# RoPE on half of each head: one row of the last tile split over GpSimd's DMA queue

## The chip, the cores and the metric

The kernel runs on one core of a Trainium2 chip. The metric is the device time of one execution in microseconds (us); the kernel before took 161.63 us, the median of three runs (161.6 to 161.7).

## What is computed

The input x is float32 of shape 16 x 512 x 16 x 64 (batch, position, head, dimension), and cos and sin are 512 x 32. Of the 64 values of a head, the first 32 (x1) are rotated and the last 32 (x2) are handed on untouched:

```python
rotated_first  = x1[..., :16] * cos[..., :16] - x1[..., 16:] * sin[..., :16]
rotated_second = x1[..., :16] * sin[..., :16] + x1[..., 16:] * cos[..., :16]
out = concatenate([rotated_first, rotated_second, x2], axis=-1)
```

Only the first 16 columns of cos and sin are used, and they depend on the position alone. x and the output have 33.55 MB each.

## The kernel before

The 8192 rows (batch times position) of 4 KB (16 heads of 64 floats) are cut into four tiles (`T`). A tile has 128 partitions, and each partition holds 16 consecutive rows (`K`), 64 KB that are contiguous in DRAM. The tiles live in `ring`, which has three slots (`NS`); tile 3 takes the slot of tile 0.

GpSimd's DMA queue first loads the two tables, 32 runs of 2 KB each (L63, L64). SyncE's queue loads tile 0, tile 1 and the first half (8 rows, `KC`) of tile 2 (L55). VectorE spreads the tables over the partitions (L73 to L83) and then rotates in place. `rotate` takes some of the 16 rows of a tile: two products (L96 into PSUM, L97 in place), a difference (L98) and a sum (L101) over the first 32 values of each head. The other 32 values ride along in the same slot, from the load to the store.

The order on the queues is the order of the program, with waits where data or a slot is needed. On SyncE: store of tile 0 (after its rotation), second half of tile 2, load of tile 3 (which waits until the store of tile 0 has landed), store of tile 1, store of tile 3. The store of tile 1 is held back by a dependency written by hand until 13 of 16 rows (`KM`) of tile 2 are rotated. On GpSimd: the two tables and the store of tile 2. Tiles 0, 1 and 3 are rotated in two halves of 8 rows, tile 2 in 8, 5 and 3 rows. The kernel ends when the store of tile 3 and the store of tile 2 have landed.

Of the kernel before, what the change touches and what calls it, by code (L numbers as in the profile page):

```python
# [1 line left out]

# [4 lines left out]


@with_exitstack
def kernel(  # L10
    ctx: ExitStack,
    tc: tile.TileContext,
    x: bass.AP,
    cos: bass.AP,
    sin: bass.AP,
    out: bass.AP,
):
    nc = tc.nc
    fp32 = mybir.dt.float32
    P = 128  # L20
    B, S, H, D = x.shape
    Q = D // 4
    HF = D // 2

    K = 16
    T = B * S // (P * K)
    PB = S // K
    REP = P // PB  # L30
    R = H * D
    NS = 3
    KC = K // 2
    KM = 13

    xf = x.rearrange("b s h d -> (b s h d)").rearrange("(t p f) -> t p f", t=T, p=P)
    of = out.rearrange("b s h d -> (b s h d)").rearrange("(t p f) -> t p f", t=T, p=P)
    cosf = cos.rearrange("(p k) j -> p (k j)", k=K)
    sinf = sin.rearrange("(p k) j -> p (k j)", k=K)

    const_pool = ctx.enter_context(tc.tile_pool(name="const", bufs=1))
    b_pool = ctx.enter_context(tc.tile_pool(name="bp", bufs=1, space=bass.MemoryType.PSUM))


    ring = const_pool.tile([P, NS, K, H, D], fp32)
    stage = const_pool.tile([P, 2, K, HF], fp32)
    spun = const_pool.tile([P, 2 * K, Q], fp32)
    packed = const_pool.tile([PB, 2 * K, Q], fp32)
    table = const_pool.tile([P, 2, K, 2, Q], fp32)

    def rows(t, lo, hi):
        return ring[:, t % NS, lo:hi].rearrange("p k h d -> p (k h d)")

    def load(t, lo=0, hi=K):
        return nc.sync.dma_start(out=rows(t, lo, hi), in_=xf[t, :, lo * R : hi * R])  # L55

    def store(t, lo=0, hi=K, queue=nc.sync):
        return queue.dma_start(out=of[t, :, lo * R : hi * R], in_=rows(t, lo, hi))  # L58


    nc.vector.memset(stage[:, :, :, 0:Q], 0.0)  # L61
    spread = stage.rearrange("(j b) t k i -> j b t (k i)", b=REP)
    nc.gpsimd.dma_start(out=spread[:, 0, 0], in_=cosf)  # L63
    nc.gpsimd.dma_start(out=spread[:, 0, 1], in_=sinf)  # L64
    load(0)
    load(1)
    load(2, 0, KC)

    PQ = PB // REP
    nc.vector.stream_shuffle(  # L73
        out=spun[:],
        in_=stage.rearrange("p t k j -> p (t k) j")[:, :, 0:Q],
        mask=[j % PQ * REP for j in range(PB)],
    )
    for q in reversed(range(REP)):
        n = PQ * (q + 1)
        nc.vector.tensor_copy(out=packed[0:n], in_=spun[q * PB : q * PB + n])  # L80

    for r in range(REP):
        nc.vector.tensor_copy(  # L83
            out=table[r * PB : (r + 1) * PB].rearrange("p t k c j -> p (t k) c j"),
            in_=packed.unsqueeze(2).to_broadcast((PB, 2 * K, 2, Q)),
        )
    C = table[:, 0].rearrange("p k c j -> p k (c j)")
    Sn = table[:, 1].rearrange("p k c j -> p k (c j)")

    def rotate(t, lo, hi):  # L90
        x1 = ring[:, t % NS, lo:hi, :, 0:HF]
        c = C[:, lo:hi].unsqueeze(2).to_broadcast((P, hi - lo, H, HF))
        s = Sn[:, lo:hi].unsqueeze(2).to_broadcast((P, hi - lo, H, HF))
        b_full = b_pool.tile([P, KC, H, HF], fp32, name="b_t")
        b_t = b_full[:, 0 : hi - lo]
        nc.vector.tensor_mul(out=b_t, in0=x1, in1=s)  # L96
        nc.vector.tensor_mul(out=x1, in0=x1, in1=c)  # L97
        nc.vector.tensor_sub(  # L98
            out=x1[:, :, :, 0:Q], in0=x1[:, :, :, 0:Q], in1=b_t[:, :, :, Q:HF]
        )  # L100
        return nc.vector.tensor_add(  # L101
            out=x1[:, :, :, Q:HF], in0=x1[:, :, :, Q:HF], in1=b_t[:, :, :, 0:Q]
        )

    rotate(0, 0, KC)
    rotate(0, KC, K)
    store(0)
    load(2, KC, K)
    load(3)
    rotate(1, 0, KC)  # L110
    rotate(1, KC, K)
    behind_loads = store(1)
    rotate(2, 0, KC)
    near = rotate(2, KC, KM)
    rotate(2, KM, K)
    store(2, queue=nc.gpsimd)

    tc.add_manual_dep(
        behind_loads.ins,
        near.ins.name,  # L120
        mybir.DependencyInfo(mybir.DependencyClass.Sync, mybir.DependencyReason.DATA),
        reason="the store follows the loads at the DMA engines",
    )
    rotate(3, 0, KC)
    rotate(3, KC, K)
    store(3)


# [1 line left out]
_INS = ['x', 'cos', 'sin']  # L130
_OUTS = [((16, 512, 16, 64), 'float32')]


# [23 lines left out]
```

## Time and profile before

| What | Value |
|---|---|
| Median of three runs | 161.63 us |
| Span of the profiled execution (first to last instruction) | 159.5 us; of this execution no time but the span is recorded |
| VectorE (DVE) busy | 112.9 us |
| GpSimd (POOL) busy | 1.9 us |
| Bytes moved by DMA | 67.24 MB, mean 422 GB/s |
| Transfers on SyncE's queue (q1) | 5 loads, 3 stores |
| Transfers on GpSimd's queue (q0) | 2 tables, 1 store |
| Store of tile 3 issued | 131.2 us, landing 27.4 us later |

The profile counts a DMA engine's work in packets. A packet is the piece of a transfer that one DMA engine carries out before it turns to another queue; its recorded time is given as a share of the time of all 16 engines in the stretch looked at. A packet is counted where it ends, so that a short stretch can show over 100%. "Landing" is the time from an issue until the transfer's completion has been counted on all its engines. A transfer's issue by an instruction and its movement by the DMA engines are thus two things: the first is shown on the issuing engine, the second in the queues.

### The profile page before, as it was taken

To read this page: it belongs to the slowest core of one execution; us is meant where nothing else is said; L and a number is where in the kernel's file an instruction comes from. 1 tells how busy PE (TensorE), PEld (TensorE's weight loads), DVE (VectorE), ACT (ScalarE), POOL (GpSimd) and SP (SyncE) were. 2 spreads that over 40 slices of the span, in tenths; PEclk is the share of its full clock that TensorE was granted. 3 is DMA by queue.
4 is the path that set the end of the run, shared out by engine and by line. 5 is a ranking of instruction groups with operands and counts; after the bars stand their busy time and mean duration, and the time that the engine had idled before them with its cause. 6 is when DMAs were issued, how large, how long until landed. Compare 5 with 4: busy or idle time off the path is not lost.

```text
span 159.5 us, 115 instructions
## 1 busy us (share of the span) xinstructions
DVE 112.9 (71%) x47; POOL 1.9 (1%) x7
## 2 busy tenths in 40 slices
DVE  1000959999999999999999999999999990000000
POOL 3000000000000000000000000010000000000000
DMA  7969979899699699699996996996996996998966
GB/s 263 542 263 542 444 345 526 362 427 526 271 493 551 263 526 526 263 395 427 493 526 263 526 526 263 526 526 263 526 526 263 526 510 279 526 427 362 526 263 263
DMA packets 1360, 67.24 MB, mean 422 GB/s; under 512 B 176, under 2 KB 176, under 8 KB 208
## 3 DMA queue, kind: packets, MB, share of 16 engines
q1 hardware_dynamic: 1152, 58.72, 85.7%
q0 software_dynamic: 208, 8.52, 12.4%
HBM read 33.69 MB, written 33.55 MB: 422 GB/s over the span
## 4 chain that ended last, share of the span: by engine, by line
DVE 61%; DMA 14%; issue 5%; DVEq 1%
DVE b_t L96 22%; DVE ring L97 22%; DMA ring<-in_x_dram 14%; DVE ring L101 10%; DVE ring L98 7%; DVEq L152 1%; DVEq L96 0%
## 5 line engine op out<-in xcount | busy, mean ns | idle before, releaser
L96 DVE TENSOR_TENSOR b_t<-ring,table 128x4096 f32<-128x4096 f32 (+2 forms) x9 | 35.6, 3959 | 2.1 <-DMA ring<-in_x_dram 1.9
L97 DVE TENSOR_TENSOR ring<-ring,table 128x4096 f32<-128x4096 f32 (+2 forms) x9 | 35.6, 3950 | 0.3
L98 DVE TENSOR_TENSOR ring<-ring,b_t 128x2048 f32<-128x2048 f32 (+2 forms) x9 | 18.4, 2050 | 0.3
L101 DVE TENSOR_TENSOR ring<-ring,b_t 128x2048 f32<-128x2048 f32 (+2 forms) x9 | 18.4, 2043 | 0.0
L73 DVE LOAD_MASK_SELECT spun<-stage x1 | 0.0, 14 | 14.4 <-DMA stage<-in_sin_dram 14.4
L83 DVE COPY table<-packed 32x1024 f32<-32x1024 f32 x4 | 2.7, 684 | 0.1
L58 POOL DMA_DIRECT2D out_dram<-ring x1 | 0.6, 559 | 101.7 <-DVE ring L101 101.7
L80 DVE COPY packed<-spun 32x512 f32<-32x512 f32 (+3 forms) x4 | 1.7, 416 | 0.1
L61 DVE MEMSET stage<- 128x512 f32 x1 | 0.5, 485 | 0.9 <-PEq L141 0.9
L73 DVE STREAM_SHUFFLE spun<-stage 128x512 f32<-128x512 f32 x1 | 0.7, 722 | 0.0
L63 POOL DMA_DIRECT2D stage<-in_cos_dram x1 | 0.6, 642 | 1.3 <-DVE stage L61 1.3
L64 POOL DMA_DIRECT2D stage<-in_sin_dram x1 | 0.5, 532 | 0.0
L141 POOL MEMSET const-bfloat16-1.0<- 128x1 bf16 x1 | 0.1, 101 | 0.0
L141 POOL MEMSET const-float32-0.0<- 128x1 f32 x1 | 0.1, 98 | 0.2 <-issue 0.2
L141 POOL MEMSET const-float32-1.0<- 128x1 f32 x1 | 0.1, 98 | 0.0
L141 POOL MEMSET const-uint8-127<- 128x1 uint8 x1 | 0.1, 98 | 0.0
## 6 DMA issues: line engine op xcount, KB each, us to landing
ring<-in_x_dram SPq DMA_DIRECT2D x2, 4096.0 KB, 40.7
stage<-in_cos_dram POOLq DMA_DIRECT2D x1, 64.0 KB, 8.9
stage<-in_sin_dram POOLq DMA_DIRECT2D x1, 64.0 KB, 13.3
ring<-in_x_dram SPq DMA_DIRECT2D x3, 28.9
out_dram<-ring SPq DMA_DIRECT2D x3, 27.4
out_dram<-ring POOLq DMA_DIRECT2D x1, 39.5
```

The lines of the kernel that those rows point to most:

```text
L58: return queue.dma_start(out=of[t, :, lo * R : hi * R], in_=rows(t, lo, hi))
L61: nc.vector.memset(stage[:, :, :, 0:Q], 0.0)
L63: nc.gpsimd.dma_start(out=spread[:, 0, 0], in_=cosf)
L64: nc.gpsimd.dma_start(out=spread[:, 0, 1], in_=sinf)
L73: nc.vector.stream_shuffle(out=spun[:], in_=stage.rearrange("p t k j -> p (t k) j")[:, :, 0:Q], mask=[j % PQ * REP for j in range(PB)],)
L80: nc.vector.tensor_copy(out=packed[0:n], in_=spun[q * PB : q * PB + n])
L83: nc.vector.tensor_copy(out=table[r * PB : (r + 1) * PB].rearrange("p t k c j -> p (t k) c j"), in_=packed.unsqueeze(2).to_broadcast((PB, ...
L96: nc.vector.tensor_mul(out=b_t, in0=x1, in1=s)
L97: nc.vector.tensor_mul(out=x1, in0=x1, in1=c)
L98: nc.vector.tensor_sub(out=x1[:, :, :, 0:Q], in0=x1[:, :, :, 0:Q], in1=b_t[:, :, :, Q:HF])
L101: return nc.vector.tensor_add(out=x1[:, :, :, Q:HF], in0=x1[:, :, :, Q:HF], in1=b_t[:, :, :, 0:Q])
L152: with _tile.TileContext(nc) as tc:
```

## The change

Row 15 of tile 3 (`LAST = K - 1`) no longer rides with the rest of its tile. SyncE loads and stores rows 0 to 14 of tile 3 alone, 60 KB per partition. The row's 16 heads are viewed as two halves (`c=2`) of 32 floats, 128 bytes each, and GpSimd's queue moves them in three transfers of 128 partitions x 16 heads:

- the untouched halves go from x to the output directly, DRAM to DRAM. This copy waits, by a dependency written by hand, for the rotation of the first half of tile 0;
- the halves to be rotated are loaded into their place in the ring. Like the rest of tile 3, this load waits until the store of tile 0 has freed the slot;
- after the rotation these halves are stored from there.

The untouched halves of row 15 have no place in SBUF any more. What VectorE does is unchanged, except that the second half of tile 3's rotation now waits for the load on GpSimd's queue also. GpSimd's order becomes: the two tables, the copy, the row's load, the store of tile 2, the row's store.

```diff
+    split = "t p (k h c d) -> t p k h c d"
+    xs = xf.rearrange(split, k=K, h=H, c=2)
+    os_ = of.rearrange(split, k=K, h=H, c=2)
+    ring_s = ring.rearrange("p n k h (c d) -> p n k h c d", c=2)
+    LAST = K - 1
...
-    rotate(0, 0, KC)
+    begun = rotate(0, 0, KC)
+    copied = nc.gpsimd.dma_start(
+        out=os_[T - 1, :, LAST, :, 1], in_=xs[T - 1, :, LAST, :, 1]
+    )
+    tc.add_manual_dep(
+        copied.ins,
+        begun.ins.name,
+        mybir.DependencyInfo(mybir.DependencyClass.Sync, mybir.DependencyReason.DATA),
+        reason="the tables go first",
+    )
     rotate(0, KC, K)
     store(0)
     load(2, KC, K)
-    load(3)
+    load(3, 0, LAST)
+    nc.gpsimd.dma_start(out=ring_s[:, 3 % NS, LAST, :, 0], in_=xs[3, :, LAST, :, 0])
...
     rotate(3, 0, KC)
     rotate(3, KC, K)
-    store(3)
+    store(3, 0, LAST)
+    nc.gpsimd.dma_start(out=os_[3, :, LAST, :, 0], in_=ring_s[:, 3 % NS, LAST, :, 0])
```

## The prediction

> **What bounds the kernel now.** I read the page first: the engines, the queues, then single stretches of the DMA view.
>
> ```profile
> span 159.5 us, 115 instructions
> DVE 112.9 (71%) x47; POOL 1.9 (1%) x7
> ...
> DMA packets 1360, 67.24 MB, mean 422 GB/s; under 512 B 176, under 2 KB 176, under 8 KB 208
> ...
> q1 hardware_dynamic: 1152, 58.72, 85.7%
> q0 software_dynamic: 208, 8.52, 12.4%
> ```
>
> VectorE is busy for 71% of the span; the two queues keep the 16 DMA engines busy for 85.7 + 12.4 = 98.1% of it. q1 is SyncE's queue, q0 is GpSimd's. The 67.24 MB leave no idle stretch, so work added to the DMA engines, or taken from them, should move the end by its own length.
>
> VectorE has room. The chain of waits runs 22 us of DMA (the first load), then VectorE without a gap, and its last rows are:
>
> ```profile
> 117.75 4.44 DVE b_t L96
> ...
> 122.22 4.43 DVE ring L97
> ...
> 126.68 2.29 DVE ring L98
> 128.97 2.20 DVEq L152
> ```
>
> VectorE ends at 131.2, and the span 28.3 us later. The last store alone is 8 packets per engine, 19.4 us at the packet time worked out below, and some 3.6 us to the end of the span; VectorE alone would thus let the span end at 154. It may be some 5 us late before it sets the end.
>
> The third view is the DMA queues of single stretches (packets, MB, share of 16 engines). From 144.5 to 146, from 7 to 8, from 157 to 158 and from 131 to 145 us:
>
> ```profile
> q1 hardware_dynamic: 12, 0.79, 121.1%
> ```
>
> ```profile
> q0 software_dynamic: 16, 0.07, 15.9%
> ```
>
> ```profile
> q1 hardware_dynamic: 8, 0.00, 0.5%
> ```
>
> ```profile
> q0 software_dynamic: 64, 3.15, 52.0%
> q1 hardware_dynamic: 64, 3.15, 51.9%
> ```
>
> First: 12 packets of 64 KB; 1.5 us x 1.211 x 16 / 12 = 2.42 us each, or 27.1 KB per us on one engine. Second: the 16 packets of a table load, one per engine, each 4 KB; 1 us x 0.159 = 0.159 us. A table has 32 runs of 2 KB, so a packet of q0 holds two runs. Third: the completion packets of the last store, a few bytes each; 1 us x 0.005 x 16 / 8 = 0.010 us. Fourth: 64 packets against 64; where both queues have work, each engine takes one packet from each in turn. That is why a small transfer lands late:
>
> ```profile
> stage<-in_sin_dram POOLq DMA_DIRECT2D x1, 64.0 KB, 13.3
> ```
>
> 64 KB took 13.3 us, since every small packet stood behind a 2.42 us packet of q1.
>
> **The change, part by part.** All of it concerns row 15 of the last tile.
>
> Removed: 4 KB per partition from a load and from a store. With 8 partitions per engine (128 over 16), that is 32 KB + 32 KB = one 64 KB packet per engine: -2.42 us. The packets that remain of these two transfers hold 60 KB, 2.27 us each.
>
> Added: three transfers on q0, each 128 partitions x 16 heads of 128-byte runs, 2048 runs, 128 per engine. Together 384 runs per engine. The copy moves in one step what was loaded and stored. In bytes the three are 48 KB per engine against the 64 KB removed.
>
> Price of a run: the trace has no 128-byte run, so I bound it.
> - Bytes alone: 128 / 27.1 KB per us = 4.7 ns. 384 x 4.7 = 1.81 us, net -0.61.
> - Packet with two runs: 0.159 us is 0.008 over its 4 KB (4.096 / 27.1 = 0.151), 4 ns per run. So 8.7 ns; 384 x 8.7 = 3.34, net +0.92.
> - A tiny write by itself: 9 to 10 ns (0.010 above; 0.3% of 1.5 us in the half after it, 9 ns). With the bytes 13.7 ns; 384 x 13.7 = 5.26, net **+2.84**.
> - The same on the reading and on the writing side, one after the other: 27.4 ns; 10.5 us, net +8.1.
>
> I take 13.7: a run of 128 bytes is far nearer to the tiny write than to the 2 KB run. The other ends stay for the range. Break-even is 2.42 / 384 = 6.3 ns.
>
> The Trainium skill, "DMA: Bandwidth & Descriptors", section "Why small descriptors are slow (HBM only)", gives about 3 cycles of overhead for every packet beside one for each 32 bytes: 7 for 4 here, so an estimate of 8.3 ns and a net of +0.8 us if every run pays it. The same page's Specifications speak against the change more strongly: below 512 bytes a transfer is said to be read, modified and written back, with no price; no run in this trace can show it.
>
> Packets: q0 merged two 2 KB runs into 4 KB. If it fills 4 KB again, 32 runs make a packet, 4 data packets and a completion per transfer and engine. I take that.
>
> The copy is issued behind the first rotation (36.4 us) and no instruction waits for its data. Its five turns at 2.42 us end near 50 to 58. Its engine time is in the sum.
>
> GpSimd's issue is not paid. Table issues took 0.64 and 0.53 us for 32 runs, the store of tile 2 0.56 for 128. At worst 0.56 / 128 = 4.4 ns a run, 9 us for 2048; at best about 0.6 us. For the first two, GpSimd has idle time until 104.6 (its wait is 101.7 us). The third is issued at 131.2 behind the store of tile 2, whose data hold q0 until about 139 and its completion until 143.5: 12 us of cover. Without that cover, up to 9 us of issue would come before the last runs.
>
> The row's load waits for the store of tile 0 (landing near 71.8), as the load of tile 3 does now. Five turns and up to 9 us of issue bring it in by about 95. The second half of tile 3's rotation now waits for it, at 117.75: 22 us of room. GpSimd's store of tile 2 stands behind this load in program order, and q0 is clear by 104.6.
>
> Loads are late by what is added ahead of them: copy and row load, 256 x 13.7 = 3.5, less 1.21 removed, +2.3 us. Tile 3's load lands at 100.7 and is wanted at 104.3: hidden. At 27.4 ns it is +5.8, and VectorE is 2.2 us late, still within its 5 us.
>
> The end: after 143.5 SyncE's store has five packets left per engine, and q0 has four data packets to place between them, so both end together. The 2.1 us from the last data (155.8) to the completion (about 157.9) stay.
>
> Sum: -2.42 + 5.26 = +2.84; span 162.3. The profiled execution is known by its span, 159.5; the median run is 161.63, 2.13 more, which I leave as it is. **Forecast: 161.63 + 2.84 = 164.5 us**; its own range, runs of 8 to 20 ns, +0.7 to +5.3: 162.3 to 166.9.
>
> **Rivals.**
> 1. Cheap runs, faster. A run costs its bytes (4.7 ns): -0.61, 161.0 us. If also the copy, which never enters SBUF, goes beside the packets of q1, only 256 runs are paid: 1.21 - 2.42 = -1.21, 160.4. It decides below 6.3 ns a run. For it: 4 KB packets ran within 5% of the full rate. Against it: that packet had two runs, not 32.
> 2. Runs that pay for both sides in series, 27.4 ns: +8.1, 169.7 us. For it: DRAM is written in 128-byte pieces at every other 128 bytes. Against it: nothing here shows reads and writes of a queue in series.
> 3. One packet per run. Then every run waits 2.42 us behind q1. From 36.5 to 120 (tile 1's store ends there, with q0 stuck) 34 runs pass; 224 of copy and row load remain and take 3.1 us alone; with 2 us of landing the half rotation starts at 125, 7.3 late. Store 3 begins at 138.5 and shares with two packets of store 2: 161.5; some 120 runs are left, 1.7 us: 163.2 in place of 155.7, +7.5, **169.1 us**. For it: each 64 KB run was a packet. Against it: the tables' 4 KB packets.
> 4. Runs of 5.4 to 7.2 ns: the change pays what it saves, 161.6 us.
>
> **Chances.** A measurement of this kernel can tell about 0.2%, 0.33 us, from no change. Forecast with its own range 0.48; rival 1 (faster) 0.22; rival 4 (same) 0.08; rival 2 or more 0.14; rival 3 0.08. Faster 0.22, same 0.08, slower 0.70. The range runs from 160.6 (between the two forms of rival 1) to 172.0 (rivals 2 and 3 inside, not both together).
>
> **What would show it.** In the profile after: SyncE's queue at 58.20 MB; the page's count of packets under 8 KB (with 4 KB counted there, as now). If merged, q0 has about 12 x 16 data packets more, and their share of the engines' time divided by 384 is the price of a run; if not, over 6000 more. VectorE's wait before the second half of tile 3 stays zero. The last completion is SyncE's or within a microsecond of it. The forecast falls if the runs take under 6.3 ns, if q0's packets are single runs, if the store of row 15 ends microseconds after SyncE's, or if q1 shows gaps.

## The result and the profile after

The changed kernel takes 162.88 us (162.75 to 163.06, three runs) against 161.63: a ratio of 1.0079, 95% interval 1.006 to 1.0099, so +1.25 us. The forecast was +2.84, 164.5 us, with the range 160.6 to 172.0. The direction held, and so did the bound and the merging of runs into packets; the size was 2.3 times too large. The profiled execution took 162.75 us, with a span of 160.6.

The page of the changed kernel, the rows that answer to those of before:

```profile
span 160.6 us, 123 instructions
DVE 112.9 (70%) x47; POOL 5.5 (3%) x10
...
DMA packets 1600, 66.98 MB, mean 417 GB/s; under 512 B 224, under 2 KB 224, under 8 KB 448
...
q1 hardware_dynamic: 1152, 57.67, 84.2%
q0 software_dynamic: 448, 9.31, 13.7%
```

q0 has 240 packets more: 3 x 16 completions and 192 with data. 6144 runs in 192 packets are 32 runs each: the runs were merged into 4 KB. q1 lost 1.05 MB, a sixteenth of a load and of a store (the prediction's 58.20 MB subtracted only one of the two; its -2.42 us has both). In engine time q0 gained 0.137 x 160.6 - 0.124 x 159.5 = 2.2 us, but q1 gave back only 0.857 x 159.5 - 0.842 x 160.6 = 1.5 us, not 2.42. That is the first hint where the price sits: partly on the packets of the other queue.

The timeline of the changed kernel from 126 us on (start, length, engine, line):

```profile
129.07 2.28 DVE L107 TENSOR_TENSOR ring<-ring,b_t 128x2048 f32<-128x2048 f32 x1
131.38 0.34 SPq L58 DMA_DIRECT2D out_dram<-ring  x1
131.64 1.17 POOL L143 DMA_DIRECT2D out_dram<-ring  x1 [26.32 <-DVE ring L107]
```

VectorE ends within 0.2 us of where it did; no wait was added before tile 3. GpSimd's issue of 2048 runs takes 1.17 us and is covered. So the loss is not a later start of the last store: the DMA work itself ends later.

The store of row 15 runs beside SyncE's store of tile 3. The DMA queues from 145 to 155 us, first before, then after:

```profile
q1 hardware_dynamic: 64, 4.19, 96.8%
```

```profile
q1 hardware_dynamic: 64, 3.93, 94.4%
q0 software_dynamic: 64, 0.26, 8.2%
```

Before, 64 packets of 64 KB take 10 x 16 x 0.968 / 64 = 2.42 us each. After, a packet of 60 KB takes 2.36, where its bytes are worth 2.27, and a q0 packet 0.205 us, where 4 KB are worth 0.151. The two surpluses, 0.09 and 0.05 us, are the price of 32 short runs.

A third part falls due before any short run moves. GpSimd issues the copy at 36.9 us, and q0's first packet of it begins only after 40. SyncE's packets that begin from 36 to 38 us, before and after:

```profile
q1 hardware_dynamic: 16, 1.05, 121.0%
```

```profile
q1 hardware_dynamic: 16, 1.05, 127.8%
```

They take 2 x 16 x 1.278 / 16 = 2.56 us each in place of 2.42, 0.14 more. In two later experiments the share is 121.0% without the copy and 127.7% with it.

For the end, one point of reading has to be put right first: the profile counts a packet where it begins, not where it ends, as was said ahead of the prediction. Before, from 0 to 2.2 us:

```profile
q1 hardware_dynamic: 16, 1.05, 144.5%
```

These 16 packets of the first load take 2.2 x 16 x 1.445 / 16 = 3.2 us each, and SyncE issues that load at 0.74 us: they cannot have ended by 2.2. Shares and lengths of packets are not touched by this, but a packet runs on after the slice in which it is counted.

The last packets of all, in slices of 0.1 us, before from 155.7 and after from 156.8:

```profile
q1 hardware_dynamic: 3, 0.20, 453.4%
```

```profile
q1 hardware_dynamic: 1, 0.06, 143.7%
q0 software_dynamic: 1, 0.00, 0.6%
```

These are the last engines to begin their last packet, three before and one after (its q0 packet there is a completion), 1.1 us later than before. The packet takes 2.42 us before and 2.30 after, so the data end near 158.2 and 159.2, some 1.0 us apart; the span grew by 1.1. The last packets began within 0.3 us of each other before (155.5 to 155.8) and within 0.7 us after (156.2 to 156.9). The completions of q1 are counted right where these packets end (157.9 to 158.3 before, 158.5 to 159.2 after).

### The profile page after: what moved, and what is told of

Read it like the earlier page. It is cut to its first block, busy times and chain, and to the rows that moved or that the text cites. A ratio compares the mean times of both kernels' runs of the same rounds, so it can differ in the third digit from the quotient of the medians.

```text
span 160.6 us, 123 instructions
## 1 busy us (share of the span) xinstructions
DVE 112.9 (70%) x47; POOL 5.5 (3%) x10
## 3 DMA queue, kind: packets, MB, share of 16 engines
q1 hardware_dynamic: 1152, 57.67, 84.2%
q0 software_dynamic: 448, 9.31, 13.7%
## 4 chain that ended last, share of the span: by engine, by line
DMA 34%; issue 31%; DVE 15%; POOLq 1%; POOL 0%; SPq 0%; DVEq 0%
DMA ring<-in_x_dram 34%; DVE b_t L102 6%; DVE ring L103 6%; DVE ring L107 3%; DVE ring L104 1%; POOLq L169 1%; POOL out_dram L58 0%; SPq L58 0%; POOLq L58 0%; DVEq L102 0%; POOLq L143 0%
## 5 line engine op out<-in xcount | busy, mean ns | idle before, releaser
L125 POOL DMA_DIRECT2D ring<-in_x_dram x1 | 1.2, 1165 | 35.2 <-DMA out_dram<-ring 35.2
L112 POOL DMA_DIRECT2D out_dram<-in_x_dram x1 | 1.2, 1170 | 34.0 <-DVE ring L107 34.0
L143 POOL DMA_DIRECT2D out_dram<-ring x1 | 1.2, 1167 | 26.3 <-DVE ring L107 26.3
L58 POOL DMA_DIRECT2D out_dram<-ring x1 | 0.6, 569 | 30.3 <-DVE ring L107 30.3
## 6 DMA issues: line engine op xcount, KB each, us to landing
ring<-in_x_dram SPq DMA_DIRECT2D x2, 4096.0 KB, 42.3
out_dram<-in_x_dram POOLq DMA_DIRECT2D x1, 256.0 KB, 12.6
```

The costliest lines, as they stand in the source:

```text
L112: copied = nc.gpsimd.dma_start(out=os_[T - 1, :, LAST, :, 1], in_=xs[T - 1, :, LAST, :, 1])
L125: nc.gpsimd.dma_start(out=ring_s[:, 3 % NS, LAST, :, 0], in_=xs[3, :, LAST, :, 0])
L143: nc.gpsimd.dma_start(out=os_[3, :, LAST, :, 0], in_=ring_s[:, 3 % NS, LAST, :, 0])
```

## The experiments

Theory 1: each 128-byte run costs a DMA engine about 9.5 ns, and the end moves by the sum, less 2.42 us. Theory 2: the price is that of small packets between large ones, whatever their runs. Theory 3: it is a price per transfer, or of the end on two queues. Each kernel was timed beside the kernel before on its own chip; that one took 161.60 us for the first four experiments, 161.53 for the next four and 161.66 for the last four. Prices per run are worked out from medians. The diffs are against the kernel before, or against the changed kernel where lines of that one are replaced or left out; "..." stands for lines not shown.

**The row whole on GpSimd's queue, no short run.**

```diff
-    copied = nc.gpsimd.dma_start(
-        out=os_[T - 1, :, LAST, :, 1], in_=xs[T - 1, :, LAST, :, 1]
-    )
...
-    nc.gpsimd.dma_start(out=ring_s[:, 3 % NS, LAST, :, 0], in_=xs[3, :, LAST, :, 0])
+    nc.gpsimd.dma_start(out=rows(3, LAST, K), in_=xf[3, :, LAST * R : K * R])
...
-    nc.gpsimd.dma_start(out=os_[3, :, LAST, :, 0], in_=ring_s[:, 3 % NS, LAST, :, 0])
+    store(3, LAST, K, queue=nc.gpsimd)
```

> Row 15 of tile 3 goes over GpSimd's queue whole, in runs of 4 KB, both ways; no copy DRAM to DRAM, no 128-byte run. Theory 1 (the price is that of the 128-byte runs, about 9.5 ns of a DMA engine each): the bytes are those of the kernel before, 161.6 to 161.9 us. Theory 2 (the price is that of a small packet between large ones, 0.30 us per 4 KB packet instead of 0.15, whatever runs are in it): 16 packets per engine at 0.15 more, 164.0 us. Theory 3 (the price is that of more transfers on GpSimd's queue and of a store that ends on two queues): two of the three transfers are left, 162.5 us.

Measured: 162.16 us, ratio 1.0034 (1.0022 to 1.0046), +0.56. Theory 2 falls (164.0). Theory 1 missed too, as it gave 161.9 at most, and so did theory 3, with 162.5. The queues of this kernel from 145 to 155 us:

```profile
q1 hardware_dynamic: 64, 3.93, 90.7%
q0 software_dynamic: 64, 0.26, 6.4%
```

Here a 60 KB packet takes 2.27 us and a 4 KB packet 0.160: with runs of 4 KB both surpluses are gone. Per packet of 32 runs the store in the changed kernel pays 2.36 + 0.205 - 2.27 - 0.160 = 0.14 us more (0.1375 before rounding), or 9.3 ns per run, (0.1375 + 0.160) / 32. The surplus on the large packet belongs to the short runs, not to the alternation. This is the row that carries theory 1.

The +0.56 looks like a wait at the end, and is not. The same kernel from 155 to 156 us, from 156 to 157.5 and from 157.5 to 159:

```profile
q1 hardware_dynamic: 16, 0.98, 226.7%
q0 software_dynamic: 16, 0.07, 15.9%
```

```profile
DMA packets 0, 0.00 MB, mean 0 GB/s; under 512 B 0, under 2 KB 0, under 8 KB 0
```

```profile
q0 software_dynamic: 64, 0.20, 32.4%
q1 hardware_dynamic: 16, 0.00, 0.6%
```

The row's store has eight packets per engine and finds five turns; the last three per engine come behind SyncE's last data. But no engine stands idle before them: SyncE's last packets begin between 155 and 156 and take 2.27 us each, which fills the stretch in which nothing is counted. (Four packets, as in the changed kernel, find their turns.) So most of the loss lies in the packets' own times. The page has 84.0% for q1 and 13.9% for q0, of a span of 160.2 us: q0 gained 0.139 x 160.2 - 0.124 x 159.5 = 2.5 us, and q1 gave back 0.857 x 159.5 - 0.840 x 160.2 = 2.1, not 2.42. That is a net 0.4 of the span's 0.7. The 16 packets of 4 KB at 0.160 in place of 0.151 make 0.14 of it; the rest is not explained.

**Rows 14 and 15 in place of row 15.**

```diff
-    LAST = K - 1
+    LAST = K - 2
...
-    nc.gpsimd.dma_start(out=ring_s[:, 3 % NS, LAST, :, 0], in_=xs[3, :, LAST, :, 0])
+    nc.gpsimd.dma_start(out=ring_s[:, 3 % NS, LAST:K, :, 0], in_=xs[3, :, LAST:K, :, 0])
...
```

> The changed kernel with rows 14 and 15 in place of row 15: the same three transfers, each twice as long. Theory 1 (the price is that of the 128-byte runs): twice the net of one row, 161.63 + 2 x 1.25 = 164.1 us. Theory 3 (a price per transfer, with runs near the price of their bytes): the saving of bytes doubles and the price doesn't, 161.9 to 162.6 us.

Measured: 164.24 us, ratio 1.0165 (1.0152 to 1.0178), +2.64: as theory 1 said, against theory 3. It fits twice the net of one row (2.5 us), but not all of it need be the runs: the row whole lost 0.56 without any.

**One transfer added to the kernel before: the copy, or a load.**

```diff
+    copied = nc.gpsimd.dma_start(
+        out=os_[T - 1, :, LAST, :, 1], in_=xs[T - 1, :, LAST, :, 1]
+    )
...
```

> The kernel before with the copy DRAM to DRAM added alone; tile 3 is still loaded and stored whole, so these bytes are written twice. 128 runs per engine come in addition. Theory 1 with one price for all three transfers (9.4 to 9.6 ns a run): +1.2 us, 162.85 us. If the copy goes beside the large packets: 161.6 to 161.8 us, and the load and the store pay nearly all. If it pays more, for both its ends lie in DRAM: 163.5 us or over.

Measured: 162.26 us, ratio 1.0051 (1.0032 to 1.007), +0.66: between its bytes alone and the one price.

```diff
+    scratch = const_pool.tile([P, H, HF], fp32, name="scratch")
...
+        extra = nc.gpsimd.dma_start(out=scratch[:], in_=xs[T - 1, :, LAST, :, 0])
...
```

> The kernel before with one more load of 2048 runs of 128 bytes into a tile that nobody reads, on GpSimd's queue behind the first rotation. Theory 1 with one price for all: +1.2 us, 162.85 us. If reading small runs is cheap and writing them to DRAM is dear: +0.6 us (their bytes), 162.25 us.

Measured: 162.72 us, ratio 1.0072 (1.0059 to 1.0085), +1.12, 8.8 ns per run. Reading short runs is not cheap.

**Four times as many runs added.** These make the price large against the scatter. All are held back until the first rotation, as the copy is; the store, which reads tile 1's slot, waits for that tile's load too and is issued at 42.95 us.

```diff
+    LAST = K - 4
...
+    copied = nc.gpsimd.dma_start(
+        out=os_[T - 1, :, LAST:K, :, 1], in_=xs[T - 1, :, LAST:K, :, 1]
+    )
...
```

> The kernel before with a copy DRAM to DRAM of the untouched halves of four rows added (8192 runs of 128 bytes, 512 per engine, one transfer); tile 3 is still stored whole over them. Theory 1a (each kind of transfer has its own price; the single copy added 0.66 us): +2.6 us, 164.2 us. Theory 1b (one price of about 9.2 ns for all runs): +4.7 us, 166.3 us. If the 0.66 us was mostly the price of one more transfer and not of its runs: 162.5 to 163.5 us.

Measured: 166.05 us, ratio 1.0278 (1.0263 to 1.0294), +4.52, 8.8 ns per run: the one price (1b), not the cheap copy.

```diff
+    extra = nc.gpsimd.dma_start(out=scratch, in_=xs[T - 1, :, K - 4 : K - 2, :, 0])
...
+    extra = nc.gpsimd.dma_start(out=scratch, in_=xs[T - 1, :, K - 2 : K, :, 0])
...
```

> The kernel before with loads of 8192 runs of 128 bytes (512 per engine, two transfers one after the other) into the tables' staging tile, which nobody reads by then. The single load added 1.12 us for 128 runs per engine. Theory 1 (a price per run, 8.8 ns): +4.5 us, 166.1 us. Bytes alone (4.7 ns), with the rest of the 1.12 us a price per transfer: 164.0 to 165.0 us.

Measured: 165.99 us, ratio 1.0272 (1.0257 to 1.0287), +4.46, 8.7 ns per run. Theory 1 held; a price per transfer is not seen.

```diff
+    LAST = K - 4
...
+    extra = nc.gpsimd.dma_start(out=os_[T - 1, :, LAST:K, :, 1], in_=ring_s[:, 1, LAST:K, :, 1])
...
```

> The kernel before with a store of 8192 runs of 128 bytes added (512 per engine, one transfer), from tile 1's slot into the rows of tile 3 that the last store overwrites later. Theory 1a (own price for each kind; what is left for the store in the changed kernel is 1.25 + 2.42 - 0.66 - 1.12 = 1.9 us for 128 runs, 15 ns each): +7.6 us, 169.2 us. Theory 1b (one price of about 9.2 ns): +4.7 us, 166.3 us. If the store's runs are as cheap as the copy's, and the rest of the changed kernel's loss lies elsewhere (its end, its waits): 164.2 us or less.

Measured: 168.55 us, ratio 1.0433 (1.0415 to 1.0451), +7.02, 13.7 ns per run: nearest to theory 1a (169.2). The trace says that this is not the price of a run alone. The queues of this kernel from 56 to 70 us, where its packets alternate with SyncE's, and from 52.5 to 54, where they follow each other:

```profile
q1 hardware_dynamic: 80, 5.24, 90.1%
q0 software_dynamic: 80, 0.33, 6.8%
```

```profile
q0 software_dynamic: 70, 0.29, 111.4%
q1 hardware_dynamic: 1, 0.00, 0.0%
```

Alternating, a q0 packet takes 14 x 16 x 0.068 / 80 = 0.19 us and a 64 KB packet 2.52, 0.10 over its 2.42: 0.29 together, 9.1 ns per run, as in the changed kernel. In a row, a q0 packet takes 1.5 x 16 x 1.114 / 70 = 0.38 us, 11.9 ns per run; 112 packets, seven per engine, begin in such a row from 52 to 54 us. Nine packets at 0.29 and seven at 0.38 are 5.3 of the 7.02 us. Another 0.8 us lies far from any short run: the added store has landed by 77.3 us, and from 102 to 104 this kernel has

```profile
q1 hardware_dynamic: 16, 1.05, 162.2%
```

These packets take 2 x 16 x 1.622 / 16 = 3.24 us each in place of 2.42; why is open. At the end the engines' last packets begin from 160.9 to 162.8 us, 1.9 us apart in place of 0.3, and the slowest engine sets the time. So 13.7 ns holds more than the runs themselves.

```diff
+    pairs = xf.rearrange("t p (k m u d) -> t p k m u d", k=K, m=H // 2, u=2)
+    extra = nc.gpsimd.dma_start(out=scratch, in_=pairs[T - 1, :, K - 4 : K - 2, :, 0])
...
+    extra = nc.gpsimd.dma_start(out=scratch, in_=pairs[T - 1, :, K - 2 : K, :, 0])
...
```

> The same bytes as the load of 8192 runs of 128 bytes, in 4096 runs of 256 bytes (256 per engine, two transfers). If the overhead belongs to the run (about 4 ns beside its bytes): 256 x (9.4 + 4.1) = 3.5 us, 165.1 us. If it belongs to the 4 KB packet or its bytes, whatever the runs: as with 128 bytes, 166.1 us. If runs of 256 bytes pay their bytes alone: +2.4 us, 164.0 us.

Measured: 165.32 us, ratio 1.0237 (1.022 to 1.0254), +3.79. Half the runs for the same bytes cost 15% less: 14.8 ns per run, of which 9.4 are bytes and 5.4 are not, against 4.0 for a run of 128 bytes. This is nearest to the 165.1 us of an overhead per run. The overhead goes mostly with the run; longer runs help, and 256 bytes are still far from free.

**The row whole on the way in only.**

```diff
-    load(3)
+    load(3, 0, LAST)
+    nc.gpsimd.dma_start(out=rows(3, LAST, K), in_=xf[3, :, LAST * R : K * R])
```

> Row 15 whole over GpSimd's queue in runs of 4 KB on the way in only; tile 3 is stored as in the kernel before. The kernel with the row whole in both directions took 162.16 us, 0.56 more than before, without one short run. If that was its end (eight packets of the row's store against five turns left, so that three or four per engine came behind SyncE's completion): the load alone costs 8 x (0.160 - 0.151) = 0.07 us, 161.6 to 161.8 us. If it was the price of 4 KB packets between large ones, paid equally by load and store: 161.85 to 161.95 us.

Measured: 162.02 us (161.79 to 163.04, twelve runs), ratio 1.0016 (1.0007 to 1.0025): +0.36 by the medians, +0.26 (0.11 to 0.40) by the ratio. The load alone costs more than the 0.07 us of its packets, and about half of the first experiment's 0.56, as if load and store paid alike. What they pay for is open.

**The three transfers on ScalarE's queue.**

```diff
-    copied = nc.gpsimd.dma_start(
+    copied = nc.scalar.dma_start(
...
-    nc.gpsimd.dma_start(out=ring_s[:, 3 % NS, LAST, :, 0], in_=xs[3, :, LAST, :, 0])
+    nc.scalar.dma_start(out=ring_s[:, 3 % NS, LAST, :, 0], in_=xs[3, :, LAST, :, 0])
...
-    nc.gpsimd.dma_start(out=os_[3, :, LAST, :, 0], in_=ring_s[:, 3 % NS, LAST, :, 0])
+    nc.scalar.dma_start(out=os_[3, :, LAST, :, 0], in_=ring_s[:, 3 % NS, LAST, :, 0])
```

> The changed kernel with its three transfers of 128-byte runs on ScalarE's DMA queue in place of GpSimd's. If runs are put into 4 KB packets there too: 162.9 us, as the changed kernel. If each run is a packet there, every one waits its turn behind SyncE's packets of 2.4 us, as rival 3 of the prediction had it: the half rotation of tile 3 is late by 7 us or more, 169 us or over.

Measured: 163.71 us, ratio 1.0125 (1.0111 to 1.0139), +2.05: neither. Its queue on the page, then from 40 to 50 us, then from 158 to 159.5:

```profile
q10 hardware_dynamic: 6192, 0.79, 3.1%
```

```profile
q1 hardware_dynamic: 128, 3.67, 85.4%
q10 hardware_dynamic: 126, 0.02, 1.0%
```

```profile
q10 hardware_dynamic: 1906, 0.24, 103.0%
q1 hardware_dynamic: 14, 0.00, 0.5%
```

On this queue each run is a packet: 6144 runs and 48 completions. Its record reads 1.5 x 16 x 1.03 / 1906 = 13.0 ns. While SyncE's queue has data, one run passes per SyncE packet (126 against 128). But they do not wait for its whole queue, as rival 3 had it. Where one of SyncE's transfers ends, most of a transfer's 2048 short runs come through at once: 1877 from 51.5 to 53 us, 1816 from 100 to 101.5, 1906 at the end. In such a row the records overlap. From 158.5 to 159 us:

```profile
q10 hardware_dynamic: 837, 0.11, 136.0%
q1 hardware_dynamic: 1, 0.00, 0.1%
```

The records add up to 136% of the engines' time, and an engine begins a run every 0.5 x 16 / 837 = 9.6 ns, not every 13.0. By the time of the whole kernel a run costs (2.05 + 2.42) / 384 = 11.6 ns.

**The changed kernel without one of its parts.**

```diff
-    copied = nc.gpsimd.dma_start(
-        out=os_[T - 1, :, LAST, :, 1], in_=xs[T - 1, :, LAST, :, 1]
-    )
...
```

> The changed kernel without the copy DRAM to DRAM: the untouched halves of row 15 of tile 3 are never written, so 256 KB of the output are left out. Theory 1c (prices from the additions of 512 runs: copy 8.8, load 8.7, store 13.7 ns a run): -2.42 + 128 x (8.7 + 13.7) = +0.45, 162.05 us. Theory 1b (one price, 9.6 ns): -2.42 + 256 x 9.6 = +0.04, 161.65 us. If the copy costs only what the single copy added, 0.66: 162.2 us.

Measured: 162.54 us, ratio 1.0052 (1.0039 to 1.0064), +0.88: above what all theories gave. Load and store cost 2.42 + 0.88 = 3.30 us here, 12.9 ns per run. Some of it is not in short runs: the large packets of tile 2's store on q0 that begin from 134 to 136 us take 2 x 16 x 1.209 / 14 = 2.76 us, against 2.45 in the changed kernel, whose row stands second:

```profile
q0 software_dynamic: 14, 0.92, 120.9%
```

```profile
q0 software_dynamic: 16, 1.05, 122.7%
```

```diff
-    nc.gpsimd.dma_start(out=os_[3, :, LAST, :, 0], in_=ring_s[:, 3 % NS, LAST, :, 0])
```

> The changed kernel without the row's store at its end: the rotated halves of row 15 of tile 3 are never written, so 256 KB of the output are left out. Theory 1c (store 13.7 ns a run): -2.42 + 128 x (8.8 + 8.7) = -0.18, 161.4 us. Theory 1b (one price, 9.6 ns): 161.65 us. If the loss of the changed kernel is mainly its end on two queues: 161.2 us or less.

Measured: 161.63 us, ratio 0.9994 (0.9983 to 1.0004), -0.03. Copy and load alone cost 2.39 us, 9.3 ns per run: as much as all the bytes saved. Without the store the change breaks even, and the store's runs are then the whole loss: 1.25 + 0.03 = 1.28 us, 10.0 ns each (from two chips). The 161.65 of one price fits better than 161.4.

No version that writes all of the output came out below the kernel before. The break-even is 6.3 ns per run, and no price from the times of a load or a store came near it.

## Why the prediction was right in direction and wrong in size

- **The bound: right.** The DMA engines stay full (84.2 + 13.7 = 97.9%), VectorE ends where it did, and added DMA work moves the end. Where VectorE waited 3.3 us for tile 3's load, in the kernel with the large store added, the DMA engines were still 83.5 + 14.3 = 97.8% busy.
- **Packets of 4 KB: right.** 192 data packets for 6144 runs. The Trainium skill, "DMA: Bandwidth & Descriptors", section "SWDGE vs HWDGE vs iDMA", says the same of GpSimd's queue: a packet is preferably at most 4096 bytes. (A single run of 64 KB is one packet on it all the same, as the prediction's fourth row shows.) On ScalarE's queue the trace shows one run per packet.
- **The price of a run: this step failed.** The prediction took the time of a completion, a tiny packet by itself (9 to 10 ns), and added the time of the run's bytes (4.7), 13.7 ns, while its next step merged 32 runs into a packet. The term 384 x 13.7 = 5.26 us measured 1.25 + 2.42 = 3.67, or 9.6 ns per run. The large additions of loads and copies gave 8.7 and 8.8; the row it had at hand for merged runs, the tables' packet of two, gave 8.7. And the sum of the two times is too large even where each run is a packet: in a row on ScalarE's queue an engine begins one every 9.6 ns, and that kernel's time gives 11.6. Only the added store came out at 13.7, with at least 0.8 of its 7.02 us far from any short run. Why the two times do not add up is open.
- **What the merged price is made of.** Only part is in the short packet's own record, 0.205 us for 32 runs or 6.4 ns each. More lies on SyncE's packet beside it, which is 0.09 us longer. From the queues before and after, the copy (42.3 to 49 us) comes to 6.8 ns per run and the row's load (76 to 80 us) to 8.2 in the same way. With 9.3 for the store the three make 3.1 us, net +0.7 on the mean engine. With the 0.14 us around the copy's issue that is +0.8, close to the 2.2 - 1.5 = 0.7 us of the profile; the slowest engine was 1.0 later.
- **The estimate from the Trainium skill.** The section "Why small descriptors are slow (HBM only)" of "DMA: Bandwidth & Descriptors" gave 8.3 ns per run and +0.8 us, nearer than my choice. But it charges the overhead per packet, and the packets here were merged; the agreement does not show that mechanism.
- **Issue, waits and end: right.** Issues took 1.17 us (estimate 0.6 to 9). The copy landed after 12.6 us and the row's load after 12.0, near 85 us, far ahead of 117.9. The row's four packets found their turns before SyncE's last. One reading was wrong: the prediction's 2.1 us from the last data to the completion are the last packet itself, which is counted at 155.8 us, where it begins. Its 3.6 us to the end of the span hold that packet too; from the end of the data (158.2) there are 1.3. The sum does not rest on either.
- **Rival 1 (cheap runs):** only the single copy came out under 6.3 ns: 0.66 us where it was added (5.2 ns, with an interval up to 8.8), and 0.37 where it was left out (0.1 to 0.8 by the ratios). Four times the copy cost 8.8 ns a run. Whether the copy is cheaper beside loads than beside stores is open. **Rival 2 (27.4 ns):** no sign. **Rival 3:** the merging rules it out on GpSimd's queue; its waiting sum would have been wrong too, as ScalarE's queue shows.

What stays open: how the price divides between the three transfers. By the medians, load and store cost 3.30 us without the copy, and load and copy 2.39 without the store, but 1.12 and 0.66 each alone. Within the intervals these four and the changed kernel still fit one price for each kind, for 128 runs about 0.9 us for the copy, 1.3 for the load and 1.8 for the store (7, 10 and 14 ns per run). The large additions of loads (8.7) do not fit that well, and the packets of the store itself show 9.3 ns. That the price depends on what runs beside it is possible, but not shown; single rounds of large packets were delayed by 0.3 and 0.8 us in two kernels, and this is as large as the differences in question.

## What to carry to other kernels

Where DMA engines are full, count runs as well as bytes: here 0.26 MB less traffic lost against 6144 runs of 128 bytes at 9.6 ns, with a break-even at 6.3. Price a run by a row of the same packaging, and look at the large packets beside it, since part of the price is recorded there. Before calling a stretch of the DMA view idle, find out from a row whether it counts packets where they begin or where they end.

## What the runs showed that I had not expected

- A short-run packet lengthens the other queue's packet: 60 KB took 2.36 us beside 32 runs and 2.27 beside one run of 4 KB.
- A stretch without a counted packet need not be idle: with the row whole none is counted from 156 to 157.5 us, and all engines are in packets of 2.27 us that began before.
- Merging depends on the queue: 32 runs per packet on GpSimd's, one on ScalarE's, which made the whole kernel 0.8 us slower than on GpSimd's (163.71 against 162.88, two chips).
- GpSimd's issue grew little with the runs: 0.56 us for 128, 1.17 for 2048, 2.78 for 8192.
